# Two decoder layers on one core: the tiles that matmuls read moved to other places in SBUF

## The chip, the cores and the metric

The kernel runs on one core of a Trainium2 chip. Its time is the device time of one launch in microseconds; the kernel before takes 1929.31 us (median of 3 runs, 1929.06 to 1930.37). The engines are called by the names of the profile: PE (TensorE's matmuls) and PEld (its weight loads), DVE (VectorE), ACT (ScalarE), POOL (GpSimd), SP (SyncE, which here only issues DMAs).

## The reference

A trunk of two decoder layers over 512 tokens with 1024 channels in float32. Each layer normalizes x, multiplies it with one wide input projection and feeds two mixers, a gated linear recurrence and a dilated sliding-window attention of 12 heads. Their projections are merged by gates, projected and added to x; then comes a gated MLP with a short causal convolution:

```
for l in range(DEPTH):
    z = rms_norm(x, ln1_g[l]) @ w_in[l]
    xr, gr, q, k, v, g_rnn, g_att = jnp.split(z, cuts, axis=-1)
    hr = rg_lru(causal_depthwise_conv(xr, ...), ...)
    y_rnn = hr * jax.nn.gelu(gr)
    y_att = dilated_attention_mixer(q, k, v, positions, ...)
    merged = sigmoid(g_rnn) * (y_rnn @ proj_rnn[l]) + sigmoid(g_att) * (y_att @ proj_attn[l])
    x = x + merged @ w_out[l]
    u = causal_depthwise_conv(rms_norm(x, ln2_g[l]) @ w_up[l], ...)
    u_gate, u_val = jnp.split(u, 2, axis=-1)
    x = x + (jax.nn.gelu(u_gate) * u_val) @ w_down[l]
```

## The kernel before

**The stream of products.** All weights pass through the core once, in 320 units of 256 rows by 512 columns (512 KB, tile wraw). Each unit is split exactly into two parts, whi (by ScalarE, L219) and wlo = wraw - whi (by VectorE, L224), and each operand of the other side is split in the same way: xh and xl are the two parts of the normalized x, eight tiles of 512 tokens each. A product is then three matmuls, high by high, high by low and low by high, in mm3 (L249 to L251). Per unit there are 2 row chunks x 4 blocks x 3 matmuls = 24 matmuls of 128x512 into four PSUM banks named acc; 320 units make 7680. The groups in order per layer are:

- N1, P1, v0, va, P2, N2, P3, P4, vb: queries, keys and values, token-major. Here whi and wlo move through the array and 128 tokens of xh or xl are loaded as weights (stationary). N1, N2 and v0 load them contiguously, the other six with a step of four tokens, 16 bytes.
- xr, gr (recurrence), ga, gn (gates), fg, fv (MLP up): channel-major. Here xh and xl move, 512 tokens at a time, and 128 columns of whi or wlo are stationary.
- pa, pr, wo, wd (the projections back): whi and wlo stationary as well, and what moves are split activations, in slots (2 KB tiles, pa) or quads (8 KB tiles of four chunks, pr, wo and wd).

**The work between.** Normalization, attention, recurrence, convolutions and gates run as chains of steps; offer() and ensure() put their steps between the matmuls by an estimate of how far each engine has come (T). The estimate counts elements and knows no addresses. There are 944 further matmuls in these chains: transposes, scores, values, the gates of the recurrence.

**Where tiles lie.** A pool hands out SBUF in the order in which tiles are first asked for. The lowest 16,384 bytes of each partition are scratch for the DMAs that GpSimd issues, the next 128 hold four constants. Then comes pool cp: xh, xl, the parameters prm, const, two small tiles posi and warm of 32 bytes each, the first two quads (x is loaded into them), ones, and bias, again of 32 bytes. So what is asked for up to bias begins on a multiple of 64 bytes, and everything large behind it 32 bytes past one. Each slot or quad keeps its place as long as the kernel runs, and is used again by whatever work takes it next. The places in the built program:

| tile | from byte | place in a line of 64 bytes | place in a line of 2048 bytes |
|---|---|---|---|
| xh (8), xl (8) | 16,512 to 49,280 | 0 | 128 |
| quads, two of 11 | 54,336 and 62,528 | 0 | 1088 |
| slots (19) | between 79,712 and 137,056 | 32 | 1888 |
| quads, nine of 11 | between 116,576 and 194,400 | 32 | 1888 |
| wraw (2), whi (3), wlo (3) | 194,400 to 227,168 | 32 | 1888 |

A matmul reads a tile from its start or from a multiple of 512 bytes into it; the six token-major groups with a step start 0, 4, 8 or 12 bytes into xh or xl. By this table the 7680 products fall into these kinds:

| groups | moves (place) | stationary (place) | products |
|---|---|---|---|
| xr, gr, ga, gn, fg, fv | xh, xl (0) | whi, wlo (32) | 3840 |
| wo, wd | quads (448 at 0, 1088 at 32) | whi, wlo (32) | 1536 |
| pa, pr | slots, quads (32) | whi, wlo (32) | 576 |
| N1, N2, v0 | whi, wlo (32) | xh, xl (0) | 576 |
| P1 to P4, va, vb | whi, wlo (32) | xh, xl with a step (0, 4, 8, 12) | 1152 |

## Time and profile before

| | |
|---|---|
| median of 3 runs | 1929.31 us |
| span of the profiled execution | 1928.1 us |
| PE busy | 1916.2 us (99%), 8624 matmuls |
| PEld busy | 1614.3 us (84%), 8624 loads |
| DVE busy | 1218.9 us (63%) |
| ACT busy | 967.7 us (50%) |
| granted TensorE clock | 1.00 |

The span runs from the first to the last instruction of the profiled execution. Matmuls are pipelined, so the duration of one (about 0.4 us) overlaps the next; how fast they follow each other is read from their starts. PEld runs beside PE. In a matmul's names, out<-in,in, the first input is the one that moves and the second the stationary one (acc<-xh,whi: xh moves).

### The profile page before, as it was taken

To read this page: it belongs to the slowest core of one execution; us is meant where nothing else is said; L and a number is where in the kernel's file an instruction comes from. 1 tells how busy PE (TensorE), PEld (TensorE's weight loads), DVE (VectorE), ACT (ScalarE), POOL (GpSimd) and SP (SyncE) were. 2 spreads that over 40 slices of the span, in tenths; PEclk is the share of its full clock that TensorE was granted. 3 is DMA by queue.
4 is the path that set the end of the run, shared out by engine and by line. 5 is a ranking of instruction groups with operands and counts; after the bars stand their busy time and mean duration, and the time that the engine had idled before them with its cause. 6 is when DMAs were issued, how large, how long until landed. Compare 5 with 4: busy or idle time off the path is not lost.

```text
span 1928.1 us, 22326 instructions
## 1 busy us (share of the span) xinstructions
PE 1916.2 (99%) x8624; PEld 1614.3 (84%) x8624; DVE 1218.9 (63%) x1781; ACT 967.7 (50%) x1683; POOL 1.9 (0%) x7
## 2 busy tenths in 40 slices
PE   8999999999999999999999999999999999999999
PEld 6899988888888888888889999888888888888887
DVE  6848877775457663577376478677644676536662
ACT  6758866663244431344366587667522444313431
POOL 0000000000000000000000000000000000000000
PEclk9999999999999999999999999999999999999999
DMA  5222223222422232222332222222224222222222
GB/s 172 93 73 87 83 67 102 84 88 98 142 99 88 96 101 91 91 92 99 121 116 85 79 99 72 78 99 82 93 98 142 88 89 97 99 98 88 98 99 88
DMA packets 66026, 185.69 MB, mean 96 GB/s; under 512 B 16928, under 2 KB 17056, under 8 KB 65920
## 3 DMA queue, kind: packets, MB, share of 16 engines
q1 hardware_dynamic: 61392, 183.59, 28.0%
q8 instruction: 67, 1.10, 0.2%
q10 hardware_dynamic: 4368, 0.17, 0.1%
q0 software_dynamic: 160, 0.50, 0.1%
q14 instruction: 39, 0.32, 0.1%
HBM read 180.00 MB, written 4.24 MB: 96 GB/s over the span
## 4 chain that ended last, share of the span: by engine, by line
PE 99%; DMA 0%; DVE 0%; ACT 0%; SPq 0%; issue 0%; ACTq 0%; DVEq 0%
PE acc L249 31%; PE acc L250 31%; PE acc L251 31%; PE at L255 2%; PE at L251 1%; PE at L250 1%; PE at L249 1%; PE y L787 1%; DMA wraw<-wst 0%; PE y L788 0%; PE y L249 0%; PE y L251 0%; PE y L250 0%; ACT slot L213 0%; ACT whi L219 0%; DVE ssq L224 0%
## 5 line engine op out<-in xcount | busy, mean ns | idle before, releaser
L219 ACT CAST whi<-wraw 128x1024 fp32r<-128x1024 f32 (+1 forms) x321 | 335.6, 1045 | 630.8 <-PE acc L250 551.4
L224 DVE TENSOR_TENSOR wlo<-wraw,whi 128x1024 fp32r<-128x1024 f32 (+1 forms) x321 | 390.3, 1216 | 279.2 <-ACT whi L219 279.1
L249 PE MATMUL acc<-xh,whi 128*128 128x512 f32 x1280 | 507.6, 397 | 0.0
L251 PE MATMUL acc<-xh,wlo 128*128 128x512 f32 x1280 | 505.6, 395 | 0.0
L250 PE MATMUL acc<-xl,whi 128*128 128x512 f32 x1280 | 505.5, 395 | 0.0
L251 PEld LDWEIGHTS acc<-xh,wlo 128*128 128x128 f32 x1280 | 239.9, 187 | 58.7
L250 PEld LDWEIGHTS acc<-xl,whi 128*128 128x128 f32 x1280 | 240.0, 188 | 57.3
L249 PEld LDWEIGHTS acc<-xh,whi 128*128 128x128 f32 x1280 | 240.0, 188 | 57.2
L250 PE MATMUL acc<-quad,whi 128*128 128x512 f32 x640 | 251.1, 392 | 0.0
L251 PE MATMUL acc<-quad,wlo 128*128 128x512 f32 x640 | 251.0, 392 | 0.0
L249 PE MATMUL acc<-quad,whi 128*128 128x512 f32 x640 | 250.4, 391 | 0.0
L249 PE MATMUL acc<-whi,xh 128*128 128x512 f32 x576 | 241.2, 419 | 7.0 <-ACT whi L219 7.0
L250 PE MATMUL acc<-wlo,xh 128*128 128x512 f32 x576 | 230.6, 400 | 0.1
L251 PE MATMUL acc<-whi,xl 128*128 128x512 f32 x576 | 229.7, 399 | 0.0
L249 PEld LDWEIGHTS acc<-whi,xh 128*128 128x128 f32 x576 | 155.8, 270 | 15.6 <-ACT whi L219 7.7
L224 DVE TENSOR_TENSOR slot<-acc,rbc 128x512 f32<-128x512 f32 x112 | 77.2, 689 | 138.7 <-PE acc L251 138.7
L250 PEld LDWEIGHTS acc<-wlo,xh 128*128 128x128 f32 x576 | 156.8, 272 | 9.0 <-DVE wlo L224 1.0
L251 PEld LDWEIGHTS acc<-whi,xl 128*128 128x128 f32 x576 | 156.0, 271 | 8.7
L249 PEld LDWEIGHTS acc<-quad,whi 128*128 128x128 f32 x640 | 120.2, 188 | 26.9
L250 PEld LDWEIGHTS acc<-quad,whi 128*128 128x128 f32 x640 | 120.2, 188 | 26.9
L251 PEld LDWEIGHTS acc<-quad,wlo 128*128 128x128 f32 x640 | 120.1, 188 | 26.4
L219 ACT CAST quad<-quad 128x512 fp32r<-128x512 f32 x80 | 49.8, 622 | 83.2 <-DVE quad L224 83.2
(137 smaller groups left out, 1947.7 us busy)
## 6 DMA issues: line engine op xcount, KB each, us to landing
wraw<-wst SPq DMA_DIRECT2D x319, 512.0 KB, 3.2
quad<-xT SPq DMA_DIRECT2D x16, 256.0 KB, 5.3
slot<-gqk SPq DMA_DIRECT2D x12, 256.0 KB, 3.6
slot<-lruw SPq DMA_DIRECT2D x8, 256.0 KB, 5.4
xdram<-quad SPq DMA_DIRECT2D x8, 256.0 KB, 3.2
quad<-xdram SPq DMA_DIRECT2D x8, 256.0 KB, 5.2
yT<-quad SPq DMA_DIRECT2D x8, 256.0 KB, 2.1
wraw<-wst SPq DMA_DIRECT2D x2, 256.0 KB, 4.9
```

What stands on the lines that cost most here:

```text
L219: nc.scalar.copy(out, src)
L224: nc.vector.tensor_tensor(out, a, b, op=op)
L249: nc.tensor.matmul(ps, rr(ah), rr(bh), start=first, stop=False)
L250: nc.tensor.matmul(ps, rr(ah), rr(bl), start=False, stop=False)
L251: nc.tensor.matmul(ps, rr(al), rr(bh), start=False, stop=last)
L255: nc.tensor.transpose(out, src, ident)
L787: nc.tensor.matmul(yp[:, o:o + 256].rearrange("p (k t) -> p k t", k=2), rr(w[:, 2, b]), rr(w[:, 0:2, b]), start=i == 0, stop=False)
```

## The change

Every tile that a matmul of the large products reads is now asked for first, in one row: xh, xl, three fixed tiles whi, three fixed tiles wlo, the 11 quads and the 19 slots. Unit u uses whi and wlo number u mod 3, where before the ring of a pool handed out the same three in turn. The small tiles follow, wraw stays in the pool ring. The scratch for DMAs goes from 16,384 to 4,096 bytes. Comments and docstrings are gone, so line numbers shift (L249 to L251 become L258 to L260).

```
+        xh = [cp.tile([128, 512], F32, name=f"xh{c}") for c in range(8)]
+        xl = [cp.tile([128, 512], F32, name=f"xl{c}") for c in range(8)]
+        whis = [cp.tile([128, 1024], F32, name=f"whi{j}") for j in range(3)]
+        wlos = [cp.tile([128, 1024], F32, name=f"wlo{j}") for j in range(3)]
+        for i in range(NQ):
+            cp.tile([128, 4, 512], F32, name="quad", tag=f"quad{i}", bufs=1)
+        for i in range(NS):
+            cp.tile([128, 512], F32, name="slot", tag=f"slot{i}", bufs=1)
...
-                hi = ring.tile([128, 1024], F32, name="whi", tag="whi", bufs=3)
+                hi = whis[u % 3]
...
-                lo = ring.tile([128, 1024], F32, name="wlo", tag="wlo", bufs=3)
+                lo = wlos[u % 3]
...
-        xh = [cp.tile([128, 512], F32, name=f"xh{c}") for c in range(8)]
-        xl = [cp.tile([128, 512], F32, name=f"xl{c}") for c in range(8)]
...
-        hi = ring.tile([128, 1024], F32, name="whi", tag="whi", bufs=3)
-        lo = ring.tile([128, 1024], F32, name="wlo", tag="wlo", bufs=3)
+        hi, lo = whis[0], wlos[0]
...
-    nc = _bacc.Bacc("TRN2", target_bir_lowering=False, num_devices=1)
+    nc = _bacc.Bacc("TRN2", target_bir_lowering=False, num_devices=1, dynamic_dma_scratch_size=4096)
```

The instructions of all five engines stay the same, one for one, in the same order and with the same waits; only addresses differ. The places after:

| tile | from byte | place in a line of 64 bytes | place in a line of 2048 bytes |
|---|---|---|---|
| xh (8), xl (8) | 4,224 to 36,992 | 0 | 128 |
| whi (3), wlo (3) | 36,992 to 61,568 | 0 | 128 |
| quads (11) | 61,568 to 151,680 | 0 | 128 |
| slots (19) | 151,680 to 190,592 | 0 | 128 |
| wraw (2) | 206,688 to 214,880 | 32 | 1888 |

## Rows read from the trace of the kernel before

**Rows 1.** The page: busy time, granted clock in 40 slices, and the chain by line.
```profile
PE 1916.2 (99%) x8624; PEld 1614.3 (84%) x8624; DVE 1218.9 (63%) x1781; ACT 967.7 (50%) x1683; POOL 1.9 (0%) x7
...
PEclk9999999999999999999999999999999999999999
...
PE 99%; DMA 0%; DVE 0%; ACT 0%; SPq 0%; issue 0%; ACTq 0%; DVEq 0%
```
**Rows 2.** PE's waits: line <- who was waited for, us, times, longest us.
```profile
PE acc L249 <- ACT whi L219: 7.0, 2, 5.5
PE at L546 <- DVE slot L224: 1.0, 1, 1.0
```
**Rows 3.** Matmul groups by form: names, shapes, count, busy us, mean ns, idle before.
```profile
L249 PE MATMUL acc<-xh,whi 128*128 128x512 f32 x1280 | 507.6, 397 | 0.0
...
L249 PE MATMUL acc<-quad,whi 128*128 128x512 f32 x640 | 250.4, 391 | 0.0
...
L249 PE MATMUL acc<-slot,whi 128*128 128x512 f32 x64 | 25.0, 390 | 0.0
```
**Rows 4.** PE in time (start us, us): first matmul of fg1, and of wd0, layer 0.
```profile
611.97 0.40 PE L249 MATMUL acc<-xh,whi 128*128 128x512 f32 x1
...
701.56 0.40 PE L249 MATMUL acc<-quad,whi 128*128 128x512 f32 x1
```
**Rows 5.** PE in time: first matmul of pr0, and of gn1 behind it, layer 0.
```profile
456.34 0.40 PE L249 MATMUL acc<-quad,whi 128*128 128x512 f32 x1
...
478.14 0.40 PE L249 MATMUL acc<-xh,whi 128*128 128x512 f32 x1
```
**Rows 6.** PE in time: first matmul of wo0, and of fg0 behind wo1, both layers.
```profile
522.34 0.39 PE L249 MATMUL acc<-quad,whi 128*128 128x512 f32 x1
...
566.71 0.40 PE L249 MATMUL acc<-xh,whi 128*128 128x512 f32 x1
...
1477.78 0.40 PE L249 MATMUL acc<-quad,whi 128*128 128x512 f32 x1
...
1522.56 0.40 PE L249 MATMUL acc<-xh,whi 128*128 128x512 f32 x1
```
**Rows 7.** PE in time, group N1 of layer 1: two matmuls 24 apart.
```profile
978.12 0.39 PE L249 MATMUL acc<-whi,xh 128*128 128x512 f32 x1
...
983.72 0.40 PE L249 MATMUL acc<-whi,xh 128*128 128x512 f32 x1
```
**Rows 8.** PE in time: fg3 behind wd1 (layer 0); wd0, fg3 (layer 1).
```profile
767.31 0.40 PE L249 MATMUL acc<-xh,whi 128*128 128x512 f32 x1
...
1657.42 0.40 PE L249 MATMUL acc<-quad,whi 128*128 128x512 f32 x1
...
1723.82 0.40 PE L249 MATMUL acc<-xh,whi 128*128 128x512 f32 x1
```
**Rows 9.** PE in time, group va of layer 1: two matmuls 24 apart.
```profile
1051.24 0.40 PE L249 MATMUL acc<-whi,xh 128*128 128x512 f32 x1
...
1056.95 0.40 PE L249 MATMUL acc<-whi,xh 128*128 128x512 f32 x1
```
**Rows 10.** Weight loads of tile xh: ns min/median/max, first and last start, forms.
```profile
L249 PEld LDWEIGHTS acc<-xh,whi x1280: 187/187/192, 251.7 to 1857.3; 128*128 128x128 f32 x183
...
L249 PEld LDWEIGHTS acc<-whi,xh x576: 186/309/330, 5.5 to 1206.4; 128*128 128x128 f32 x192
```
**Rows 11.** POOL in time, DVE in time, and the DMA issues: tile const.
```profile
1.91 0.54 POOL L432 DMA_DIRECT2D const<-cst  x1
...
22.07 0.22 DVE L235 TENSOR_SCALAR ones<-const 128x128 fp32r<-128x128 f32 x1
...
const<-cst POOLq DMA_DIRECT2D x1, 352.0 KB, 5.5
```

## The prediction, made before the change was run

> **What bounds the kernel now.** I read the page's busy time and chain first, then TensorE's waits, then the matmul groups by form, and last the starts of single matmuls in the list in order of time. [...] The waits [rows 2] show 8.0 us in which TensorE waited for anybody, 7.0 of it on two occasions for the first weights. So nothing but the pace of the matmul stream sets the time, and of its 8624 matmuls 7680 are the products of 128x512 into acc. VectorE (63%) and ScalarE (50%) are never what TensorE waits for after the start.

> The change leaves that stream as it is, instruction by instruction, and gives tiles other addresses. So the one question is whether a matmul's pace hangs on where its tiles lie. The groups by form [rows 3] say yes: the same instruction on the same shape takes 397 ns with moving xh and stationary whi, 390 with moving slot, and 391 with moving quad. These durations overlap, so I take the pace from starts. In groups fg1 to fv2, moving xh/xl (byte 0 of a 64-byte line, by the table of places above) against whi/wlo (byte 32), 384 matmuls go from 611.97 to 701.56: 89.59/384 = 233.3 ns each [rows 4]. In pr0, moving quads at byte 32 against whi/wlo at byte 32, 96 go from 456.34 to 478.14: 227.1 ns [rows 5]. Two stages of one code settle that it is the place and not the kind of work: wo0 and wo1 run over quads in both layers, but one matmul in three reads a quad at byte 0 in layer 0 (44.37 us for 192, 231.1 ns), two in three in layer 1 (44.78 us, 233.2 ns) [rows 6]. And it is not that byte 0 is slow for what moves: in the token-major group N1 the roles are turned, whi/wlo (byte 32) move and xh/xl (byte 0) are stationary, and 24 matmuls take 5.60 us, 233.3 ns again [rows 7]. So both pairings that differ (0 with 32, 32 with 0) cost 233.3, the one that agrees (32 with 32) costs 227.1, a step of 6.2 ns. [...] I take 227.1, the row of the pair that is alike, since the two unlike pairs cost the same whichever operand sits at byte 0: that speaks for agreement, not for one place being good.

> [...]

> **The change part by part.** After it every contiguous read of a product starts at byte 0 of a 64-byte line, and 6528 of the 7680 products read both operands so.
> - 3840 products move xh/xl (groups xr to gn, fg and fv): 233.3 to 227.1, 3840 x 6.2 ns = 23.8 us.
> - 1536 products of wo and wd read quads, some at byte 0 and most at byte 32. wo now takes 231.1 and 233.2 [rows 6]: 192 x 4.0 + 192 x 6.1 ns = 1.9 us. wd0 and wd1 take 65.75 us for 288 in layer 0 (701.56 to 767.31, 228.3 ns) [rows 4, 8] and 66.40 us in layer 1 (1657.42 to 1723.82, 230.6 ns) [rows 8]; for all eight wd groups I take the middle, 229.4: 1152 x 2.3 = 2.7 us.
> - 576 products of pa and pr are at 227.1 already: 0.
> - 576 products of N1, N2 and v0, byte 32 against byte 0: 576 x 6.2 = 3.6 us.
> - 1152 products of the other token-major groups load xh/xl with a step of 16 bytes. They go at 237.9 ns (24 in 5.71 us) [rows 9], and their weight load takes 309 ns in the median where a contiguous one takes 187 [rows 10]: the load starts with the matmul before it and by its 122 ns more sets the pace. The change makes its read no shorter, so I take 0; ends: the 10.8 ns down to 227.1, 12.4 us, and a loss of a step, 7.1 us.
> - The remaining 944 matmuls (transposes, scores, values, gates) are small, or 96 of the large form: 0, within 96 x 6.2 = 0.6 us either way.
> - Scratch of 4 KB instead of 16: it serves the three loads that GpSimd issues. The largest, const, is issued at 1.91 us and lands 5.5 us later, 7.4; its first reader is at 22.07 [rows 11]. A delay under 14 us is covered; beyond that TensorE would wait for the norm, one for one. I take 0.
> - VectorE and ScalarE read and write the moved tiles too. Were they slower by some nanoseconds, TensorE's lack of waits [rows 2] is the cover; were they slower by a third, VectorE's 63% would near the whole and the cover be gone.

> Sum: 23.8 + 1.9 + 2.7 + 3.6 = 32.0 us off the span of 1928.1, 1896.1. The median of the runs, 1929.31, stands 1.2 above the span; so 1897. With the stream 1.7% faster the other engines' shares rise to 64% and 51%, so nothing is late next but TensorE itself.

> **The rivals.**
> - A line's start is worth a step by itself. If a stream that starts at byte 32 always pays a step for the half line that it wastes, 32 with 32 holds one too many, and 0 with 0 is a step below, 220.9. For it: a moving tile of 2 KB at byte 32 touches 33 lines, at byte 0 32. Against it: moving at byte 0 is no faster than moving at byte 32 when the other operand differs [rows 4, 7]. The 6528 contiguous products take 232.0 ns on average now (4416 at 233.3, 1536 at 230.1, 576 at 227.1); 6528 x 11.1 = 72.5 us, so 1857. [...]
> - Byte 0 is the bad place. If any read that starts a line at the same moment as the other reader's costs the step, and only 32 with 32 escapes, every product takes 233.3: for it, every row with a byte 0 in it is at 233.3. Against it: the cost would need one operand at byte 0 to be as bad as two. Price: 6528 x 1.3 = 8.5 us more, 1938. It decides from 232.0 ns for 0 with 0: above that the kernel is slower.
> - The step is not of these 64 bytes: distance or neighbourhood of tiles makes it, and moving all by whole lines changes little. For it: the slow pairs are xh, xl and two early quads, which all lie low in memory, with whi and wlo at its top. Against it: the quads of pr0 and wo lie between, and the roles turned give the same 233.3. Time 1929. [...]

> **How the numbers follow.** Forecast (alike is alike, 227.1): 56%, 1897, its own range 1885 to 1901 (the strided products' gain below, a ragged stage above). One step lower or more: 24%, three quarters of it near 1857, the rest lower. Nothing changes: 10%, 1927 to 1932. Byte 0 is bad: 10%. What a measurement of this kernel tells from no change is 0.2%, 3.9 us; all of the first two cases is faster than that, so faster 80%, same 11% (a little of the last case), slower 9%. The range takes in the case near 1857 with some of the strided loss or gain, and no change: 1845 to 1931.

> **What would show it.** Right: in the profile after, the mean duration of acc<-xh,whi falls from 397 to about 390, fg1 to fv2 take 87.2 us instead of 89.6, pr0 keeps 21.8, and wo takes the same in both layers. The strided groups keep 238 ns and their weight load 309. Wrong upwards: pr0 slows to 22.4 while fg stays. Wrong downwards: pr0, whose pairs were alike before, gets faster too. Waits of TensorE on const or ones near 22 us would show the scratch.

## The result and the profile after

The changed kernel takes 1894.25 us (median of 4 runs, 1893.97 to 1894.81) against 1929.62 for the kernel before on the same chip (4 runs, 1929.06 to 1930.37): a ratio of 0.982, interval 0.981 to 0.983. The forecast was 1897. The profiled execution's span fell from 1928.1 to 1893.0 us, by 35.1 where the sum of the prediction said 32.0.

The page of the kernel after, with the same parts as [rows 1]:

```profile
span 1893.0 us, 22326 instructions
...
PE 1881.1 (99%) x8624; PEld 1613.3 (85%) x8624; DVE 1218.9 (64%) x1781; ACT 967.1 (51%) x1683; POOL 1.9 (0%) x7
...
PEclk9999999999999999999999999999999999999999
...
PE 97%; ACT 2%; DVE 1%; DMA 0%; issue 0%; SPq 0%; DVEq 0%
```

TensorE's busy time falls by 35.1 us, the whole difference. The counts are the same, the granted clock is 1.00 in both, and VectorE and ScalarE are busy for as long as before: 1218.9 us again, and 967.1 for 967.7. Only the pace of the matmuls has changed. TensorE's waits in the kernel after, to be read against [rows 2] (line <- who was waited for, us, times, longest us):

```profile
PE acc L258 <- ACT whi L228: 7.9, 2, 6.0
PE at L264 <- ACT slot L222: 0.2, 1, 0.2
```

The waits sum to 8.1 us, against 8.0 before: the first weights are waited for 0.9 longer, the wait of 1.0 for the norm's tile (L546 before) is gone, and one of 0.2 for ScalarE's slot, at L264, is new. The chain that ended last now goes through ScalarE and VectorE (2% and 1%) until it enters TensorE's line at 73.14 us, at that new wait: in this opening stretch ScalarE's work ends about when TensorE needs it, and holds it up by 0.22 us in all. The groups by form (names, shapes, count, busy us, mean ns), against [rows 3]:

```profile
L258 PE MATMUL acc<-xh,whi 128*128 128x512 f32 x1280 | 500.3, 391 | 0.0
...
L258 PE MATMUL acc<-quad,whi 128*128 128x512 f32 x640 | 249.0, 389 | 0.0
...
L258 PE MATMUL acc<-slot,whi 128*128 128x512 f32 x64 | 24.9, 389 | 0.0
```

The product of xh, 397 ns before, has joined the others. The pace itself stands in the starts (first column). Below, in order of time: pr0 and gn1 behind it [rows 5], wo0 and fg0 in layer 0 [rows 6], fg1, wd0 and fg3 in layer 0 [rows 4, 8], two starts of N1 that lie 24 matmuls apart [rows 7], two of va that do [rows 9], and wo0 and fg0 in layer 1 [rows 6]:

```profile
450.41 0.39 PE L258 MATMUL acc<-quad,whi 128*128 128x512 f32 x1
...
472.17 0.39 PE L258 MATMUL acc<-xh,whi 128*128 128x512 f32 x1
...
515.69 0.39 PE L258 MATMUL acc<-quad,whi 128*128 128x512 f32 x1
...
559.21 0.39 PE L258 MATMUL acc<-xh,whi 128*128 128x512 f32 x1
...
603.21 0.39 PE L258 MATMUL acc<-xh,whi 128*128 128x512 f32 x1
...
690.25 0.39 PE L258 MATMUL acc<-quad,whi 128*128 128x512 f32 x1
...
755.53 0.39 PE L258 MATMUL acc<-xh,whi 128*128 128x512 f32 x1
...
954.77 0.39 PE L258 MATMUL acc<-whi,xh 128*128 128x512 f32 x1
...
960.21 0.39 PE L258 MATMUL acc<-whi,xh 128*128 128x512 f32 x1
...
1033.34 0.40 PE L258 MATMUL acc<-whi,xh 128*128 128x512 f32 x1
...
1038.98 0.40 PE L258 MATMUL acc<-whi,xh 128*128 128x512 f32 x1
...
1453.40 0.39 PE L258 MATMUL acc<-quad,whi 128*128 128x512 f32 x1
...
1496.92 0.39 PE L258 MATMUL acc<-xh,whi 128*128 128x512 f32 x1
```

The contiguous stretches shown now run at one pace: pr0 21.76/96, wo 43.52/192 in both layers, fg1 to fv2 87.04/384, wd0 and wd1 65.28/288, N1 5.44/24, all 226.7 ns. The products with a step go at 5.64/24 = 235.0 ns where they went at 237.9. Their weight loads have not changed, as the view of tile xh shows (ns min/median/max), against [rows 10]:

```profile
L258 PEld LDWEIGHTS acc<-xh,whi x1280: 187/188/192, 250.0 to 1822.9; 128*128 128x128 f32 x183
...
L258 PEld LDWEIGHTS acc<-whi,xh x576: 186/308/330, 6.0 to 1187.0; 128*128 128x128 f32 x192
```

Start to start, added up over the whole trace by kind, the 35 us are about: xh and xl moving 24.4; quads of wo, wd and pr 5.4; N1, N2 and v0 1.4; the products with a step 2.7; the stretch of a norm's matmuls at L546 1.4; small matmuls 0.4. (Where kinds meet, 0.1 or 0.2 goes to either by the way of counting.) The first matmul starts 0.56 later (6.02 for 5.46).

### The profile page after: what moved, and what is told of

The parts are those of the page before. It is cut to its first block, busy times and chain, and to the rows that moved or that the text cites. A ratio compares the mean times of both kernels' runs of the same rounds, so it can differ in the third digit from the quotient of the medians.

```text
span 1893.0 us, 22326 instructions
## 1 busy us (share of the span) xinstructions
PE 1881.1 (99%) x8624; PEld 1613.3 (85%) x8624; DVE 1218.9 (64%) x1781; ACT 967.1 (51%) x1683; POOL 1.9 (0%) x7
## 4 chain that ended last, share of the span: by engine, by line
PE 97%; ACT 2%; DVE 1%; DMA 0%; issue 0%; SPq 0%; DVEq 0%
PE acc L258 31%; PE acc L259 30%; PE acc L260 30%; PE at L264 2%; PE at L260 1%; PE at L259 1%; PE at L258 1%; ACT junk L222 1%; PE y L794 1%; DMA wraw<-wst 0%; ACT whi L228 0%; ACT slot L222 0%; PE y L795 0%; PE y L258 0%; PE y L260 0%
## 5 line engine op out<-in xcount | busy, mean ns | idle before, releaser
L258 PE MATMUL acc<-xh,whi 128*128 128x512 f32 x1280 | 500.3, 391 | 0.0
L260 PE MATMUL acc<-xh,wlo 128*128 128x512 f32 x1280 | 498.2, 389 | 0.0
L259 PE MATMUL acc<-xl,whi 128*128 128x512 f32 x1280 | 498.2, 389 | 0.0
L260 PEld LDWEIGHTS acc<-xh,wlo 128*128 128x128 f32 x1280 | 240.3, 188 | 50.3
L258 PEld LDWEIGHTS acc<-xh,whi 128*128 128x128 f32 x1280 | 240.3, 188 | 48.9
L258 PE MATMUL acc<-quad,whi 128*128 128x512 f32 x640 | 249.0, 389 | 0.0
L260 PE MATMUL acc<-quad,wlo 128*128 128x512 f32 x640 | 249.0, 389 | 0.0
L258 PE MATMUL acc<-whi,xh 128*128 128x512 f32 x576 | 239.9, 416 | 7.9 <-ACT whi L228 7.9
L260 PE MATMUL acc<-whi,xl 128*128 128x512 f32 x576 | 228.6, 397 | 0.0
L258 PEld LDWEIGHTS acc<-whi,xh 128*128 128x128 f32 x576 | 155.8, 271 | 15.9 <-ACT whi L228 8.6
L260 PEld LDWEIGHTS acc<-whi,xl 128*128 128x128 f32 x576 | 155.8, 270 | 7.9
L260 PEld LDWEIGHTS acc<-quad,wlo 128*128 128x128 f32 x640 | 120.1, 188 | 25.0
L258 PEld LDWEIGHTS acc<-quad,whi 128*128 128x128 f32 x640 | 120.1, 188 | 24.9
```

Source lines behind the costliest of these rows:

```text
L258: nc.tensor.matmul(ps, rr(ah), rr(bh), start=first, stop=False)
L259: nc.tensor.matmul(ps, rr(ah), rr(bl), start=False, stop=False)
L260: nc.tensor.matmul(ps, rr(al), rr(bh), start=False, stop=last)
```

## The experiments

The change does several things at once: it makes the places of the operands alike, puts them at one absolute place, puts the tiles in one row, and shrinks the scratch. The letters in the expectations are theories. A is the forecast's: alike within a line of 64 bytes is what counts. B and C are its rivals, an absolute place and a longer line or another arrangement. D, formed after the first runs, is agreement within 256 bytes. All places below are bytes within a line; "pace" is ns from start to start of a 128x512 product.

**Part of the change undone: whi and wlo moved by 32 bytes (whi32).** Edit of the kernel after:

```
         xl = [cp.tile([128, 512], F32, name=f"xl{c}") for c in range(8)]
+        cp.tile([128, 8], F32, name="pad")
...
         wlos = [cp.tile([128, 1024], F32, name=f"wlo{j}") for j in range(3)]
+        cp.tile([128, 8], F32, name="pad2")
```

> The changed kernel, with whi and wlo alone moved 32 bytes on (byte 32 of a 64-byte line; xh, xl, quads and slots stay at byte 0). Theory A (the two operands have to agree within the line): all 6528 contiguous products become unlike, 226.7 to 233.3 ns, 43 us more than the change, 1937 us, so slower than the kernel before; pr0 too goes from 21.8 to 22.4 us. Theory B (what moves has to start at byte 0 of the line, the weights do not matter): xr to fv, pr, wo, wd keep 226.7 ns, only N1, N2, v0 slow, 1898 us. Theory C (what counts is that the tiles lie one behind the other): nothing changes, 1894 us.

Measured: 1937.25 us (4 runs, 1936.48 to 1938.56), ratio 1.004, interval 1.0025 to 1.0055. TensorE's starts in this run, pr0 and gn1, then fg1 and wd0, as above:

```profile
456.01 0.40 PE L260 MATMUL acc<-quad,whi 128*128 128x512 f32 x1
...
478.42 0.40 PE L260 MATMUL acc<-xh,whi 128*128 128x512 f32 x1
...
613.28 0.40 PE L260 MATMUL acc<-xh,whi 128*128 128x512 f32 x1
...
702.88 0.39 PE L260 MATMUL acc<-quad,whi 128*128 128x512 f32 x1
```

Both stretches are at 233.3 to 233.4 ns (22.41/96, 89.60/384). Six tiles shifted by 32 bytes cost 43 us and take back the whole gain and more, with the row and the scratch as in the change. pr0, which was alike before and is unlike here, is now slow as well.

**All tiles moved by 32 bytes together (all32).** Edit of the kernel after:

```
+        cp.tile([128, 8], F32, name="pad")
         xh = [cp.tile([128, 512], F32, name=f"xh{c}") for c in range(8)]
```

> The changed kernel with all matmul tiles (xh, xl, whi, wlo, quads, slots) moved on by 32 bytes, alike among themselves at byte 32. Theory A (agreement): 226.7 to 227.1 ns for every contiguous product, 1894 to 1897 us. Theory B (byte 0 is the good place): 233.3 ns, 1937 us. Theory C (one behind the other): 1894 us.

Measured: 1894.85 us (4 runs, 1893.74 to 1895.19), ratio 0.982, interval 0.980 to 0.983. fg1 and wd0:

```profile
603.16 0.39 PE L259 MATMUL acc<-xh,whi 128*128 128x512 f32 x1
...
690.20 0.39 PE L259 MATMUL acc<-quad,whi 128*128 128x512 f32 x1
```

87.04/384 = 226.7 ns with both operands at byte 32 of a 64-byte line. Byte 0 is neither good nor bad; what counts here is the relation of the two operands.

**Alike within 64 bytes, in the old order (pad).** One tile of 32 bytes in the kernel before shifts all that is asked for behind bias, so every large tile begins at byte 0 of a 64-byte line. Nothing else moves:

```
         bias = cp.tile([128, 2], F32, name="bias")
+        cp.tile([128, 8], F32, name="pad")
```

> The kernel before with one line more, a tile of 32 bytes behind bias, so that nine quads, slots, wraw, whi and wlo go from byte 32 to byte 0 of a 64-byte line; order of tiles, places in the 2 KB line (128, 1088, 1920) and the 16 KB of scratch stay as they were. Theory A (agreement within 64 bytes is all): 226.7 ns everywhere, 1894 us as the whole change. Theory C (one behind the other, the same place of a 2 KB line, is needed): 1929 us, or in between.

Measured: 1899.40 us (4 runs, 1898.66 to 1899.91), ratio 0.9845, interval 0.983 to 0.986: most of the gain, and 5 us short of the change. fg1 and wd0, then wo0 and fg0 of layer 1:

```profile
602.93 0.39 PE L249 MATMUL acc<-xh,whi 128*128 128x512 f32 x1
...
689.97 0.39 PE L249 MATMUL acc<-quad,whi 128*128 128x512 f32 x1
...
1453.98 0.39 PE L249 MATMUL acc<-quad,whi 128*128 128x512 f32 x1
...
1498.97 0.39 PE L249 MATMUL acc<-xh,whi 128*128 128x512 f32 x1
```

fg1 to fv2 run at 226.7, but wo of layer 1 at 44.99/192 = 234.3, slower than before the pad (233.2, [rows 6]), although each of its reads starts at byte 0 of a 64-byte line. What sets it apart is that two in three of its matmuls read one of the two early quads: these start at byte 64 of a 256-byte line, all other tiles at byte 128. So theory A, as the forecast had it, is too weak. (Two thirds at 233.3 and one at 226.7 would be 231.1; the 3 ns beyond that, where the place changes from one matmul to the next, no run explains.) A line of 2 KB is not needed either: xh starts at byte 128 of one and whi at byte 1920, and their pace is 226.7.

**The scratch alone (scratch).** Edit of the kernel before:

```
-    nc = _bacc.Bacc("TRN2", target_bir_lowering=False, num_devices=1)
+    nc = _bacc.Bacc("TRN2", target_bir_lowering=False, num_devices=1, dynamic_dma_scratch_size=4096)
```

> The kernel before with 4 KB of DMA scratch and nothing else: all tiles move down by 12288 bytes, their places in 64-byte and 2 KB lines stay. Theory A and C: 1929 us. If the scratch had a part in the gain: below 1927 us.

Measured: 1929.35 us (10 runs, 1929.19 to 1931.38), ratio 1.0001, interval 0.999 to 1.001. It has no part in the gain.

**Three maps of places (map16, map4, map2k).** Here the eight xh (and xl) tiles get four places, one for each pair of chunks, and the three whi (and wlo) tiles one each, so that each unit of 24 products has one place for what moves and one for what is stationary, and one run shows up to twelve pairs. Edit of the kernel after, in map2k (map16: MQ 0, 4, 8, 12 and SQ 0, 4, 8; map4: MQ 0, 1, 2, 6 and SQ 0, 2, 12, both in 4-byte elements and with 64 bytes of padding per tile):

```
+        MQ, SQ = (0, 16, 32, 64), (0, 16, 48)
+        xh = [cp.tile([128, 576], F32, name=f"xh{c}")[:, MQ[c // 2]:MQ[c // 2] + 512] for c in range(8)]
+        xl = [cp.tile([128, 576], F32, name=f"xl{c}")[:, MQ[c // 2]:MQ[c // 2] + 512] for c in range(8)]
+        whis = [cp.tile([128, 1088], F32, name=f"whi{j}")[:, SQ[j]:SQ[j] + 1024] for j in range(3)]
+        wlos = [cp.tile([128, 1088], F32, name=f"wlo{j}")[:, SQ[j]:SQ[j] + 1024] for j in range(3)]
```

> The changed kernel with other places for xh, xl (row chunks 0-1, 2-3, 4-5, 6-7 at byte 0, 16, 32, 48 of a 64-byte line) and for whi, wlo (ring place 0, 1, 2 at byte 0, 16, 32): one run shows 12 pairs in fg and fv, and three (byte 0 against 0, 16, 32) in pr and wd. Theory A in its strict form: 226.7 ns where both are equal, 233.3 ns in all others. In a graded form (the cost grows with the distance): 226.7 at 0, about 230 at 16 and 48, 233.3 at 32. If only the half of the line counts (32 bytes): 226.7 for 0 with 16 and 32 with 48 too.

> As the run with steps of 16 bytes, with finer ones: xh, xl at byte 0, 4, 8, 24, whi, wlo at byte 0, 8, 48. Strict agreement: 226.7 ns for 0 with 0 and 8 with 8 alone, 233.3 ns elsewhere. If lines of 16 bytes count: 226.7 for 0, 4, 8 against 0 and 8, 233.3 for 24 and 48 against any. Graded by distance: between the two, growing to 24 bytes.

> The changed kernel with xh, xl 0, 64, 128 or 256 bytes further on and whi, wlo 0, 64 or 192 bytes, each tile with a pad behind it, so that places in the 2 KB line differ while all stay at byte 0 of a 64-byte line. Theory A (64 bytes): 226.7 ns in all 12 pairs, 1894 us. Theory C (the same place of a 2 KB line): 226.7 ns only where they agree, up to 233.3 elsewhere, about 1920 us.

Measured, one run each: 1925.79 us (map16), 1935.40 (map4), 1920.50 (map2k). The first two were ill laid out: the padding of 64 bytes makes each tile step by 64 within a 256-byte line, so the pairs differ there as well, and nearly all units go at 230 to 239 ns, also those that are alike within 64 bytes. Of themselves they decide nothing. In map2k every tile is at byte 0 of a 64-byte line and only the place in the 256-byte line differs. Two units of it, each from its first matmul to that of the next unit, with moving and stationary at bytes 128 and 128, then 128 and 192:

```profile
609.63 0.39 PE L259 MATMUL acc<-xh,whi 128*128 128x512 f32 x1
...
615.07 0.39 PE L259 MATMUL acc<-xh,whi 128*128 128x512 f32 x1
...
631.65 0.40 PE L259 MATMUL acc<-xh,whi 128*128 128x512 f32 x1
...
637.25 0.40 PE L259 MATMUL acc<-xh,whi 128*128 128x512 f32 x1
```

5.44/24 = 226.7 and 5.60/24 = 233.3 ns. Over the run, moving less stationary modulo 256: 0 gives 226.7 to 228.7 for whole units, 64 gives 229, 128 gives 232.8, 192 gives 233.4. This settles it against the 64-byte line, and against one of 128 bytes too. The time is what theory C gave, but not by its rule: the units whose operands lie 256 bytes apart, and so at different places of a 2 KB line, end at 226.7 ns as well.

Whole units of alike pairs spread up to 228.7 because the pace takes some products to settle. Behind a unit of an unlike pair, up to the first ten products take 224 to 236 ns each; after them every alike unit of this run, but for the first of the kernel, goes at 226.7.

**Alike within 256 bytes, in the old order (pad256).** Edit of the kernel before, with the 4 KB scratch of run scratch for room:

```
         warm = cp.tile([128, 1], F32, name="warm")
+        cp.tile([128, 16], F32, name="pad0")
...
         bias = cp.tile([128, 2], F32, name="bias")
+        cp.tile([128, 56], F32, name="pad1")
```

> The kernel before with two pads (64 bytes behind warm, 224 behind bias; 4 KB of scratch to make room): every matmul tile at byte 128 of a 256-byte line, though in the old order, two quads at 1152 and all else at 128 of a 2 KB line. Theory D, from the runs with pads (the operands have to agree within a line of 256 bytes): 226.7 ns everywhere, wo and wd too, 1894 us. Theory C (one behind the other, or the same place of 2 KB): wo and wd stay uneven as in the run with one pad, 1899 us.

Measured: 1893.80 us (4 runs, 1893.66 to 1893.91), ratio 0.981, interval 0.980 to 0.983: all of the change's gain by two small pads. The stage that pad left slow, wo of layer 1:

```profile
1452.15 0.39 PE L249 MATMUL acc<-quad,whi 128*128 128x512 f32 x1
...
1495.67 0.39 PE L249 MATMUL acc<-xh,whi 128*128 128x512 f32 x1
```

43.52/192 = 226.7 ns, with tiles in the old order and two quads at another place of the 2 KB line (1152) than the rest (128). That the tiles lie one behind the other, and that each is at the same place of 2 KB, adds nothing that shows.

**What each difference costs (map256, mapfine).** The same edit as in map2k, with MQ, SQ = (0, 16, 32, 48), (0, 8, 40), and (0, 1, 4, 16), (0, 2, 60); the tiles begin a multiple of 256 bytes apart.

> The changed kernel with all tiles on multiples of 256 bytes apart, xh, xl of row chunks 0-1, 2-3, 4-5, 6-7 read 0, 64, 128, 192 bytes further on, whi, wlo of ring place 0, 1, 2 read 0, 32, 160 bytes further on: the differences (moving less stationary) take all eight multiples of 32 in 256. Theory D: 226.7 ns at 0 alone; by the run before about 229 at +64, 233 at 128 and 192, and 233 at 32 and 224; open are 96 and 160. Theory A (64 bytes): 226.7 at 0, 64, 128, 192, and 233.3 at the other four.

> As the run with multiples of 32, with differences of 4 to 80 bytes: xh, xl read 0, 4, 16, 64 bytes further on, whi, wlo 0, 8, 240 bytes. Theory D in its strict form: 226.7 ns at 0 alone and 233 at 4 already. In a graded form: near 227 up to 16 bytes and rising. If some small lead of one operand is better than none: below 226.7 at 4, 8 or 16 to either side, and a kernel with that lead would beat the changed one.

Measured, one run each: 1929.99 and 1923.67 us. Two starts 24 matmuls apart in map256 (moving 64, stationary 32), and in mapfine (132 and 136):

```profile
606.12 0.39 PE L259 MATMUL acc<-xh,whi 128*128 128x512 f32 x1
...
611.72 0.39 PE L259 MATMUL acc<-xh,whi 128*128 128x512 f32 x1
```

```profile
615.62 0.40 PE L259 MATMUL acc<-xh,whi 128*128 128x512 f32 x1
...
621.32 0.39 PE L259 MATMUL acc<-xh,whi 128*128 128x512 f32 x1
```

5.60/24 = 233.3 and 5.70/24 = 237.5 ns. The settled pace (from the start of the 14th to that of the 23rd product, in the units that no other work breaks), by moving less stationary modulo 256:

| difference, bytes | contiguous products, ns | run |
|---|---|---|
| 0 | 226.7 | both |
| 4 / 8 / 16 / 20 | 237 (233 in three units of N1, N2 and v0) / 233 / 228 or 232 / 238 | mapfine |
| 32 / 64 / 96 | 233 / 229 / 233 | map256 |
| 32 / 64 / 80 | 232 / 229 or 233 / 230 | mapfine |
| 128 / 160 / 192 / 224 | 232 / 234 / 233 / 233 | map256 |
| 248 / 252 | 231 / 237 (232 in one unit) | mapfine |

No difference goes below 226.7. The difference is not all: 16 bytes cost about 1.6 or 5 ns by where the pair lies (128 with 112, 144 with 128), and one unit with 112 and 144 went at 226.7, though 224 gives 233 in map256. Nor do the two places fix the pace of an unlike pair. In mapfine the fourth units of gr1 and of fg1 in layer 0 both have moving at 192 and stationary at 128; their first matmuls and those of the next units:

```profile
354.89 0.39 PE L259 MATMUL acc<-xh,whi 128*128 128x512 f32 x1
...
360.38 0.40 PE L259 MATMUL acc<-xh,whi 128*128 128x512 f32 x1
...
626.89 0.40 PE L259 MATMUL acc<-xh,whi 128*128 128x512 f32 x1
...
632.49 0.39 PE L259 MATMUL acc<-xh,whi 128*128 128x512 f32 x1
```

5.49/24 = 228.8 against 5.60/24 = 233.3 ns: two of the eleven such units take the pace that this pair has in map256, nine the other. What decides between them, and what lies beneath the 256 bytes, stays open; alike pairs show one settled pace, 226.7, in the kernel after and in all three maps.

For products whose weights have a step, map256 shows another order, from one to six units each: about 234 ns at a difference of 96, 235.5 at 160, 236.5 at 0 and 32 (235.1 at 0 in the kernel after), 238 at 192 and 224, 239 to 240 at 64 and 128.

**The best place for the products with a step (lead96, after_again).** In the kernel after, whi and wlo of the units of P1 to P4, va and vb are written and read 96 bytes further on. after_again is the kernel after, unchanged, on the same chip:

```
+        whis = [cp.tile([128, 1088], F32, name=f"whi{j}") for j in range(3)]
+        wlos = [cp.tile([128, 1088], F32, name=f"wlo{j}") for j in range(3)]
+        lead = [24 if g[1][0] == "P" or g[1] in ("va", "vb") else 0 for g in GROUPS for _ in range(g[3] // 2)]
...
+                hi = whis[u % 3][:, lead[u]:lead[u] + 1024]
...
+                lo = wlos[u % 3][:, lead[u]:lead[u] + 1024]
...
-        hi, lo = whis[0], wlos[0]
+        hi, lo = whis[0][:, 0:1024], wlos[0][:, 0:1024]
```

> The changed kernel, but in the units of the six token-major groups that load weights with a step (P1 to P4, va, vb) whi and wlo are read 96 bytes further on (same tiles, pad of 256 bytes behind them); all other products keep equal places. The run with multiples of 32 showed 233.5 ns there at a difference of 96 against 235.0 in the changed kernel for whole units without other work between. Theory D for contiguous products: they keep 226.7. So 1152 products at 1.5 ns less, 1.7 us (up to 3.2 ns less, 3.7 us, by the rows of that run itself): 1891 to 1893 us. If the rows with a step do not set the pace there: 1894 us.

> The changed kernel once more, on the chip of the run with the lead of 96 bytes, as its measure: 1894 us.

Measured: 1892.92 us (4 runs, 1892.48 to 1893.23) against 1894.36 (5 runs, 1893.51 to 1894.82); ratios to the kernel before 0.9809 (0.9795 to 0.9823) and 0.9815 (0.9801 to 0.9829). The first matmul of va in layer 1, and that of P2 behind its 96 products, in lead96 and in after_again:

```profile
1025.29 0.57 PE L259 MATMUL acc<-whi,xh 128*128 128x512 f32 x1
...
1047.86 0.40 PE L259 MATMUL acc<-whi,xh 128*128 128x512 f32 x1
```

```profile
1026.22 0.57 PE L258 MATMUL acc<-whi,xh 128*128 128x512 f32 x1
...
1048.95 0.40 PE L258 MATMUL acc<-whi,xh 128*128 128x512 f32 x1
```

22.57/96 = 235.1 against 22.73/96 = 236.8 ns. Over the whole trace the products with a step that follow each other go at 233.6 against 235.1 ns, 1.7 us in sum. The times differ by 1.4 us and the runs' ranges don't overlap, but the intervals of the two ratios do: this is the fastest version measured, by less than the 0.2% that the prediction took as its bound, and it is the pace in the trace that shows the gain.

## Why the prediction was right, and where not

One more row of the kernel before bears on this, to be read between the two of [rows 5]: the first matmul of pr0's second unit.

```profile
461.82 0.39 PE L249 MATMUL acc<-quad,whi 128*128 128x512 f32 x1
```

And two pairs of rows from the opening of N1 in layer 0: the sixth product and the 11th before the change, then the sixth and the 16th after it.

```profile
10.38 0.63 PE L251 MATMUL acc<-whi,xl 128*128 128x512 f32 x1
...
12.51 0.43 PE L250 MATMUL acc<-wlo,xh 128*128 128x512 f32 x1
```

```profile
11.19 0.63 PE L260 MATMUL acc<-whi,xl 128*128 128x512 f32 x1
...
15.46 0.57 PE L258 MATMUL acc<-whi,xh 128*128 128x512 f32 x1
```

- **Nothing but the matmuls' pace sets the time: right.** All 35.1 us are TensorE's busy time; the other engines' work is as long as before.
- **Alike is alike: right, shown by whi32 and all32.** 0 with 0 and 32 with 32 take the same 226.7 ns, 0 with 32 233.3. The value taken, 227.1, was that of pr0 [rows 5], and it is an average over the settling of the pace. By the row above, pr0's first unit, behind the unlike pairs of gn0, took 5.48/24 = 228.3 ns and the other three 16.32/72 = 226.7. The step is 6.6 ns, where the forecast counted 6.2. The sign "pr0 gets faster too" came true by these 0.04 us, without a lower step behind it.
- **3840 products of xh and xl: 23.8 forecast, 24.4 measured.** At 233.3 to 226.7 all of them would give 25.6; xr0 and gr0, where small matmuls stand between the products, gave 0.33 to 0.38 us a group for 0.64 in the other groups, 1.1 less in sum. Two small errors partly cancel.
- **wo and wd: 4.6 forecast, 5.3 measured (5.4 with pr).** 1536 products at 0.4 ns below the assumed end make 0.6; wo takes the same time in both layers, as was to show.
- **N1, N2 and v0: 3.6 forecast, 1.4 measured.** The step is there (233.3 to 226.7 in N1), but N1 of layer 0 opens the kernel. Its first 24 products, with the second wait for weights among them, took 11.70 us in this execution (from 6.02) and 10.34 before (from 5.46); in after_again, the same changed kernel, they took 10.71 (from 5.75). So 1.0 us of it is scatter between executions of one kernel. The rows of the opening show what scatters: the products there follow each other at 426 to 427 ns, five of them before (2.13/5), ten after (4.27/10) and eight in after_again (3.41/8, from 10.50 to 13.91). After one more of 0.27 to 0.40 us they follow at 0.22 to 0.24 us; the trace's record of the granted clock, 1.00, begins at 12.6 us before and at 15.8 after. What changes the pace there no run shows. Five products more than before at 0.2 us each are 1.0 of the 1.4 us that the opening lost. The rest is missing where waits and small matmuls break the stream: v0 gave 0.29 us in layer 0 and 0.56 in layer 1. The wait for the first weights varies too, from 6.6 to 7.9 us over all the runs; no experiment was made on it.
- **Products with a step: 0 forecast, 2.7 gained.** This is the step of the sum that failed. The argument was that the weight load, 309 ns for 187, sets their pace and does not get shorter. It does not (308), and yet the pace went from 237.9 to 235.0: the load is not the only thing that sets it. Their pace too hangs on the places: over whole traces it is 237.6 ns before the change (whi less xh 224 modulo 256), 235.1 after it (0), 236.6 in whi32 (32) and 233.6 in lead96 (96), another best difference than that of the contiguous products.
- **Scratch: 0 forecast, shown by its own run.** const lands after 6.3 us for 5.5 and its first reader starts at 22.02 for 22.07: the cover was there.
- **The line of 64 bytes: wrong, without effect on the sum.** The prediction read the step as one of a 64-byte line. In its rows the difference of xh (128) and whi (96) is 32 modulo 64 and modulo 256 alike, so they could not tell the two lines apart. The third rival said that it was not of these 64 bytes, and as to the line it was right; it was wrong that the time would stay, since the change makes all tiles alike modulo 2048, and so modulo 256. That the sum held with the wrong line is thus luck of this change's layout. What it cost shows in the run pad, which the 64-byte line puts at the time of the change and which ends 5 us above it.
- **The rivals.** A step lower for 0 with 0 (1857) and a bad byte 0 (1938) both fall: 0 with 0 goes at 226.7, as 32 with 32 does. Nothing in the runs speaks for the times below 1857 that the chances count with the first of them: no settled pace of a contiguous product is below 226.7.
- **The place of the weights counts: right.** In whi32, moving whi and wlo alone by 32 bytes takes the products from 226.7 to 233.3 ns. In map256, pairs 32 and 64 bytes apart cost 6.6 and 2.3 ns.

Why the pace hangs on the two places no run shows. The traces do show where the time goes: in fg1 to fv2 each load starts about 3 ns after the start of the matmul before its own and takes 187 to 188 ns in both kernels, and from its end to the next matmul pass 43.2 ns before the change and 35.6 after. The load is not stretched; the next matmul starts later.

## What to carry to other kernels

When TensorE is never kept waiting, compare the same instruction's start-to-start time between stages; where one shape runs at two paces, tabulate the byte places of both operands before anything else. For float32r products of 128x512 with a weight load before each, put the moving and the stationary tiles at the same place modulo 256 bytes: two pads, and the room for them that the smaller scratch gave, did it here for 1.9% with no tile reordered. It is one form on one kernel that was measured; other shapes and types were not. And before trusting a line length, look for a pair of rows that tells it from the next longer one: agreement modulo 64 fitted every row of contiguous products in the kernel before, and was not the rule.
